# State-space slots with their own fixed order on TensorE, and decay sums brought by DMA instead of made by matmuls

## Chip, core and metric

The kernel runs on one core of a Trainium2 chip. The metric is the device time of one execution in microseconds (us); lower is better. A core has five engines with a queue of instructions each: TensorE (PE, with weight loads as PEld), VectorE (DVE), ScalarE (ACT), GpSimd (POOL) and SyncE (SP), which here only issues DMAs. Each works off its queue in order, and waits for others through semaphores.

## What is computed

Two layers over 1024 latent and 256 context positions of width 1024: gated windowed attention, then a gated bidirectional state-space mixer (SSD), each with modulated normalization and a residual. The change touches only the second. For each of 8 groups (4 heads of 64 channels each, a state of 128) it projects, convolves over 5 neighbours, applies silu, and scans in 8 chunks of 128 positions, in both directions, from states that the context leaves behind:

```python
def ssd_chunk_pass(xdt, da, bm, cm, h0, want_y):
    a_cs = jnp.cumsum(da, axis=2)
    a_last = a_cs[:, :, -1]
    decay_to_end = jnp.exp(a_last[:, :, None] - a_cs)
    states = jnp.einsum('bcsgn,bcsgr,bcsgrp->bcgrpn', bm, decay_to_end, xdt)
    ...
    diff = a_cs[:, :, :, None] - a_cs[:, :, None, :]
    lmat = jnp.exp(jnp.where(lower, diff, -jnp.inf))
    cb = jnp.einsum('bcqgn,bcsgn->bcqsg', cm, bm)
    y_diag = jnp.einsum('bcqsg,bcqsgr,bcsgrp->bcqgrp', cb, lmat, xdt)
    y_off = jnp.einsum('bcqgn,bcgrpn,bcqgr->bcqgrp', cm, h_prev, jnp.exp(a_cs))
```

`da` is the step size times a negative rate, so `lmat` holds, for each pair of positions of a chunk, how much of one has decayed by the other: the decays. Both directions are added, with a skip term, multiplied by silu(z), normalized within the group and projected back to width 1024.

## The kernel before

A product of two float32 matrices is made of three matmuls of rounded halves (high x high, high x low, low x high). Products of the scan itself run in plain float32, which the trace shows as two matmul instructions for each in the program.

The method `ssd` starts with `ssd_consts`: step sizes, their running sums `acs` in both directions and logarithms of step sizes, all with 64 rows (2 directions x 32 heads); these go to DRAM (`acs_d`, and `v_d` with the logarithm minus the sum), split in two halves by `rows`, and, transposed chunk by chunk, to SBUF.

Then come 64 **slots**, one for each chunk of each group. A slot of group g makes, on TensorE: the score matrix `pcb` (C times B, 128x128); the inter-chunk part `po`, from the forward state `hf` and the stored backward state `hb`; the update `S` of `hf`; the diagonal part `yd` (4 matmuls, one for each head, with the decays times the scores `M` as weights); and two transpositions of the finished rows of the slot before (the tail), which go to DRAM as `uN`. Beside its own work a slot holds a share of **front(g+1)**: the projections of the next group, four weight tiles of 128 channels (B, x, x, C: `bT`, two `cacc`, `cT`) of 48 matmuls of 512 columns, 24 of 256 columns for the context (not for C), and 192 matmuls of 256 columns for z. In group 7, with no next group, the fill is the output projection `ssd_out`.

`fill(x)` runs front until a share of its estimated cost is spent; `SEGS` sets the shares. What follows a projection (5 conv taps on ACT and DVE, tanh, product, and for B and x the transpositions `natural` back into PSUM with ACT copies) is put into a list, `post`, of which one step is taken for each 0.5 us of estimated matmul time; the transpositions are held back by `LATE` further microseconds of it. `states(g+1)` makes the states of the next group from its context and then the backward states, chunk by chunk, each with a matmul into the one buffer `psD`, a DVE addition and POOL products (`xw`, `decay`); `tick()` takes one step of it, three times a slot.

The **decays** of slot n+1 are made in slot n. SP loads 12 rows of `acs_d` and `v_d` into `rraw` (three DMAs), ACT rounds them into `rrow`, and for each half (2 heads) two matmuls of 256 columns add sums and logarithms for both directions into PSUM; DVE's `copy_predicated` picks the direction by position (`before`), and ACT's Exp writes `M`.

The order in which the program is written is not the order of the queues: a scheduler with a timing model of its own places each engine's instructions as it takes them to become ready. What is printed below are the functions that the change touches, as they stood.

Of the kernel before, what the change touches and what calls it, by code (L numbers as in the profile page):

```python
# [9 lines left out]
F32 = mybir.dt.float32  # L10
BF16 = mybir.dt.bfloat16
F32R = mybir.dt.float32r
# [33 lines left out]
    cacc=2, cctx=1, bT=2, cT=2, xn4=4, xn2=1, bn4=4, bn2=1, sz=2, xw=2, hf=2, hx=2, M=2, y2=1, xs=1, uT=2, pj2=2, psX=3, sk=2, dg=2,  # L46
# [13 lines left out]
LATE = 3.0  # L60
SEGS = (1.5, 2.0, 2.0, 2.2, 2.2)
# [42 lines left out]
class Kernel:  # L104
# [762 lines left out]
    def ssd_consts(self, p):  # L867
# [18 lines left out]
        self.dtb = t(p, [P, NCH, 32], F32, "dtb")  # L886
        self.eal = t(p, [P, 64, NT], F32, "eal")

        self.acs_d = t(dr, [2, 64, LAT], F32, "acs")
        self.v_d = t(dr, [2, 64, LAT], F32, "vrow")  # L890
# [28 lines left out]
        for lo, n, chunks in ((0, 768, (0, 1, 2, 3, 8, 9)), (768, 512, (4, 5, 6, 7))):  # L919
# [24 lines left out]
            def rows(dst, src):  # L944
                h = t(q, [64, 512], F32R, "rowh", 2)
                l = t(q, [64, 512], F32R, "rowl", 2)
                nc.scalar.copy(h, src[:, :512])
                nc.vector.tensor_sub(l, src[:, :512], h)
                for x, y in enumerate((h, l)):
                    nc.sync.dma_start(dst[x, :, chunks[0] * P : chunks[0] * P + 512], y.bitcast(F32))  # L950

            rows(self.acs_d, acs)
# [11 lines left out]
            rows(self.v_d, ln)  # L964
# [6 lines left out]
            for b, c in enumerate(chunks):  # L971
                sl = slice(b * P, (b + 1) * P)
                pt = t(ps, [P, 256], F32, "psX")
                nc.tensor.transpose(pt[:, 0:64], dd[:, sl], self.ident[:64, :64])
                nc.scalar.copy(self.dtdec[:, c, :], pt[:, 0:64])
                if c < NCH:
                    nc.tensor.transpose(pt[:, 64:128], acs[:, sl], self.ident[:64, :64])
# [16 lines left out]
    def silu(self, raw, acc):  # L994

        nc = self.nc
        return [lambda: nc.scalar.activation(raw, acc, AF.Tanh),
                lambda: nc.vector.scalar_tensor_tensor(acc, in0=raw, scalar=1.0, in1=acc, op0=ALU.add, op1=ALU.mult)]

    def front(self, g, st, post, first=None):  # L1000
# [31 lines left out]
        def natural(raw, acc, dst, o, n):  # L1032
# [12 lines left out]
            return [(LATE, steps)]  # L1045
# [9 lines left out]
        for n, (x, kind) in enumerate(tiles):  # L1055
# [4 lines left out]
            if nat:  # L1060
# [6 lines left out]
                post.extend(self.taps(x, raw, acc, 0, CTX, CTX) + self.silu(raw, acc) + natural(raw, acc, [(st[nat[0]][2], 0, 2)], nat[1], 2))  # L1067
# [46 lines left out]
    def ssd(self, c0):  # L1114
# [11 lines left out]
        rraw = t(ps2, [32, 6, P], F32, "rraw")  # L1126
        rrow = t(ps2, [P, 6, P], F32R, "rrow")
        nc.sync.dma_start(rraw, a["rrow"].rearrange("p (r n) -> p r n", r=6))
        nc.vector.memset(rrow.bitcast(F32), 0.0)
# [60 lines left out]
        def load_rows(n):  # L1190
            g, c = divmod(n, NCH)
            cs = slice(c * P, (c + 1) * P)
            ar = self.acs_d.rearrange("h (d k) n -> (h d) k n", d=2)[:, 4 * g : 4 * g + 4, cs]
            nc.sync.dma_start(rraw[0:4, :4], ar)
            for d in range(2):
                nc.sync.dma_start(rraw[4 + 8 * d : 12 + 8 * d, 4 + d], self.v_d[:, hd(d, g), cs])

        def round_rows(n):
            nc.scalar.copy(rrow[:32], rraw)
            if n + 1 < G * NCH:  # L1200
                load_rows(n + 1)

        def decays(n, M, half):

            o = t(ps, [P, 512], F32, "psX").rearrange("p (d r n) -> p d r n", d=2, r=2)
            for d in range(2):
                nc.tensor.matmul(o[:, d], rrow[:, 4 + d], rrow[:, 2 * half : 2 * half + 2], start=True, stop=True)
            nc.vector.copy_predicated(o[:, 0], self.before.unsqueeze(1).broadcast_to([P, 2, P]), o[:, 1])
            nc.scalar.activation(M[:, 2 * half : 2 * half + 2], o[:, 0], AF.Exp)

        def slot(n, st, M, fill, tick, last):

            g, c = divmod(n, NCH)
            cs = slice(c * P, (c + 1) * P)
            xc = X(st, c).rearrange("p (r h) -> p r h", r=R)
            if n + 1 < G * NCH:
                round_rows(n + 1)
            pcb = t(ps, [P, 512], F32, "psX")[:, :P]
            nc.tensor.matmul(pcb, st["bT"][:, cs], st["cT"][:, cs], start=True, stop=True)
            po = t(ps, [P, 512], F32, "psX")  # L1220
            nc.tensor.matmul(po[:, :256], st["cT"][:, cs], flat(st["hf"]), start=True, stop=True)
            nc.tensor.matmul(po[:, 256:], st["cT"][:, cs], flat(st["hb"][c]), start=True, stop=True)
            nc.vector.tensor_tensor(M, M, pcb.unsqueeze(1).broadcast_to([P, R, P]), op=ALU.mult)
            if c < NCH - 1:
                S = t(ps, [P, 512], F32, "psX")
                hn = t(ps2, [P, R, HP], F32, "hf")
                decay(hn, st["hf"], g, c, 0)
                nc.tensor.matmul(S[:, :256], B(st, c), flat(st["xw"]), start=True, stop=True)
                nc.vector.tensor_add(hn, hn, S[:, :256].rearrange("p (r h) -> p r h", r=R))
                st["hf"] = hn  # L1230
            y2 = t(ps2, [P, 2, R, HP], F32, "y2")
            nc.vector.tensor_tensor(y2, po.rearrange("p (d r h) -> p d r h", d=2, r=R),
                                    self.eacs[:, c, :].rearrange("p (d q) -> p d q", d=2)[:, :, 4 * g : 4 * g + 4].unsqueeze(3).broadcast_to([P, 2, R, HP]), op=ALU.mult)
            fill(0)
            xs = t(ps2, [P, R, HP], F32, "xs")
# [3 lines left out]
            nc.vector.scalar_tensor_tensor(sk, in0=self.dtb[:, c, 4 * g : 4 * g + 4], scalar=dg, in1=self.dsk[:, 4 * g : 4 * g + 4], op0=ALU.mult, op1=ALU.add)  # L1239
            y = ys[n % 2]  # L1240
            yf = y[:, :256]
            yv = yf.rearrange("p (r h) -> p r h", r=R)
            nc.gpsimd.tensor_tensor(xs, xc, sk.unsqueeze(2).broadcast_to([P, R, HP]), op=ALU.mult)  # L1243
            nc.gpsimd.tensor_tensor(yv, y2[:, 0], y2[:, 1], op=ALU.add)
            nc.gpsimd.tensor_tensor(yv, yv, xs, op=ALU.add)
            yd = t(ps, [P, 512], F32, "psX")
            for r in range(R):
                nc.tensor.matmul(yd[:, r * HP : (r + 1) * HP], M[:, r], X(st, c)[:, r * HP : (r + 1) * HP], start=True, stop=True)
            if self.tail is not None:
                self.tail(t(ps, [P, 512], F32, "psX"))  # L1250
            fill(1)
            nM = None
            if n + 1 < G * NCH:
                nM = t(ps2, [P, R, P], F32, "M")
                decays(n + 1, nM, 0)
# [3 lines left out]
            nc.scalar.activation(y2.rearrange("p d r h -> p (d r h)")[:, :257], y[:, :257], AF.Square, scale=1.0 / 16.0, accum_out=ss)  # L1259
            nc.gpsimd.tensor_tensor(ss, ss, self.half, op=ALU.pow)  # L1260
            fill(2)
            if nM is not None:
                decays(n + 1, nM, 1)
            nc.scalar.activation(yf, yf, AF.Copy, scale=ss)
            if c < NCH - 2:
                st["xw"] = xweight(st, g, c + 1, 0)
            tick()
            fill(3)
            tick()
            fill(4)  # L1270
            tick()

            def tail(pt):
# [6 lines left out]
            self.tail = tail  # L1280
            return nM
# [3 lines left out]
        load_rows(0)  # L1285
# [14 lines left out]
        M = t(ps2, [P, R, P], F32, "M")  # L1300
        round_rows(0)
        for half in range(2):
            decays(0, M, half)
        st["xw"] = xweight(st, 0, 0, 0)
        self.tail = None
        with ExitStack():
            for g in range(G):
# [3 lines left out]
                else:  # L1311
                    cf.close()
                    post.flush()
                    work, total = self.ssd_out(self.pool("out", ctx=c0, side="right"), [(p, [P, 2, 512], F32, "xn4")] * 4, p, ps2, post), OUT * 0.85
                spent = 0.0
                chain = None

                def run(until):
                    nonlocal spent
# [6 lines left out]

                def tick():
                    nonlocal chain
                    if g < G - 1 and 1 in nst:
                        chain = chain or states(g + 1, nst)  # L1330
                        next(chain, None)

                for c in range(NCH):
                    def fill(x):
                        run(total * (c + sum(SEGS[: x + 1]) / sum(SEGS)) / NCH)
                    M = slot(g * NCH + c, st, M, fill, tick, g == G - 1)
                if g < G - 1:
                    run(1e9)
                    while 1 not in nst or not nst["sz"]:
                        post.pop()  # L1340
                    chain = chain or states(g + 1, nst)
                    for _ in chain:
                        pass
                    nst["xw"] = xweight(nst, g + 1, 0, 0)
                    st = nst
            self.tail(t(ps, [P, 512], F32, "psX"))
# [222 lines left out]
def layout(i):  # L1569
# [34 lines left out]
    rr = np.zeros((32, 6, P), np.float32)  # L1604
    for x in range(4):
        for r in range(R):
            rr[4 + 4 * x + r, r] = 1.0
        rr[x, 4 + x % 2] = 1.0
    d["rrow"] = rr.reshape(32, -1)
# [30 lines left out]
```

## Time and profile before

| | |
|---|---|
| median of 3 runs | 1858.76 us (1854.27 to 1859.07) |
| the profiled execution | 1859.22 us, span of its trace 1857.5 us |
| attention layer, to the first matmul of the first front | to about 753 us |
| first front, states and constants | about 753 to 870 us |
| slots of groups 0 to 6 | about 870 to 1630 us |
| slots of group 7, between matmuls of the output projection | about 1630 to 1770 us |
| rest of the output projection, final norm | 1770 to 1857 us |
| granted TensorE clock, whole run | 0.985 |

In the profile a row of a group ends with busy time, mean duration, the engine's idle time just ahead of these instructions and what ended it. In a timeline a row is start, duration, engine, line, operation, written tile and tiles read; in square brackets the idle time before it. A matmul starts before the one ahead of it has ended, so the cost of a matmul on TensorE is the distance from start to start, not its duration.

### The profile page before, as it was taken

Reading aid. Unit: us, or ns where it says so; the run is one execution under the profiler, and the core shown is the slowest. Engines: PE = TensorE matmul, PEld = TensorE weight load, DVE = VectorE, ACT = ScalarE, POOL = GpSimd, SP = SyncE. Lnnn points to the kernel's source line nnn. Section 1 sums busy time; section 2 is a strip of 40 time slices with the busy share of each in tenths; the row PEclk is TensorE's granted clock in tenths of the full one; section 3 lists DMA queues with packets and bytes.
Section 4 is the critical chain, followed back from the end, with each engine's and each line's share of the span. In section 5 each row is a group of like instructions: output and inputs, shape, how many; then the busy total and the mean of one; then the engine's idle time right before and its main releaser. Section 6 shows DMA issues by size and latency. Waiting matters only on the chain. (4 is left out here: it accounts for less than half of the span.)

```text
span 1857.5 us, 29739 instructions
## 1 busy us (share of the span) xinstructions
PE 1779.2 (96%) x10684; PEld 1539.4 (83%) x10684; DVE 1175.8 (63%) x2208; ACT 902.6 (49%) x1858; POOL 732.1 (39%) x1007
## 2 busy tenths in 40 slices
PE   6999999999999999889999999999999999999997
PEld 4797877788898787668898898989889898988886
DVE  3564438877787665773766657576665757754743
ACT  3522336677788664652444435344443534543532
POOL 2441137654466466003352443525244352532411
PEclk9999999999999999989999999999999999999998
DMA  7767866443354445221111111111111111433552
GB/s 293 279 165 252 263 179 153 105 118 96 88 137 120 129 125 191 64 61 36 30 45 47 34 47 34 48 33 40 52 33 47 34 47 35 156 109 95 175 162 71
DMA packets 145491, 196.30 MB, mean 106 GB/s; under 512 B 15392, under 2 KB 84896, under 8 KB 144320
## 3 DMA queue, kind: packets, MB, share of 16 engines
q1 hardware_dynamic: 111280, 175.76, 29.8%
q0 software_dynamic: 34064, 18.65, 5.6%
q8 instruction: 84, 1.38, 0.3%
q14 instruction: 63, 0.52, 0.1%
HBM read 158.73 MB, written 35.92 MB: 105 GB/s over the span
## 5 line engine op out<-in xcount | busy, mean ns | idle before, releaser
L226 PE MATMUL pj<-uH,wh 128*128 128x256 f32 (+1 forms) x652 | 232.3, 356 | 6.4 <-DVE xn L1528 1.9
L228 PE MATMUL pj<-uH,wl 128*128 128x256 f32 (+1 forms) x652 | 219.5, 337 | 0.0
L227 PE MATMUL pj<-uL,wh 128*128 128x256 f32 (+1 forms) x652 | 219.3, 336 | 0.0
L1148 POOL TENSOR_TENSOR xw<-xn,dtdec 128x256 f32<-128x256 f32 x144 | 105.9, 738 | 209.4 <-PE psD L1171 100.9
L1073 PE MATMUL pj<-uH,wh 128*128 128x512 f32 x512 | 172.7, 407 | 1.1 <-ACT xn L1040 1.1
L1073 PE MATMUL pj<-uH,wl 128*128 128x512 f32 x512 | 172.0, 405 | 0.0
L1073 PE MATMUL pj<-uL,wh 128*128 128x512 f32 x512 | 168.6, 399 | 0.0
L214 POOL TENSOR_TENSOR wl<-wr,wh 128x512 fp32r<-128x512 f32 x92 | 121.3, 1322 | 94.4 <-ACT wh L212 91.4
L1098 PE MATMUL pj<-wh,uH 128*128 128x256 f32 x512 | 154.0, 301 | 0.0
L702 DVE TENSOR_TENSOR pl<-pt,ph 128x512 fp32r<-128x512 f32 x168 | 114.2, 687 | 60.5 <-ACT ph L701 59.8
L1098 PE MATMUL pj<-wh,uL 128*128 128x256 f32 x512 | 150.8, 294 | 0.0
L1098 PE MATMUL pj<-wl,uH 128*128 128x256 f32 x512 | 150.4, 294 | 0.0
L226 PEld LDWEIGHTS pj<-uH,wh 128*128 128x128 f32 x652 | 124.2, 190 | 28.6 <-issue 7.8
L676 DVE CUSTOM_DVE_ANT_0 sm<-S,mask,nsink 128x640 f32<-128x640 f32 (+2 forms) x160 | 118.9, 771 | 33.8 <-PE S L673 19.7
L1277 ACT ACTIVATE uT<-psX,nw 128x128 f32<-128x128 f32 x128 | 47.0, 367 | 189.0 <-PE psX L1276 188.0
L228 PEld LDWEIGHTS pj<-uH,wl 128*128 128x128 f32 x652 | 123.7, 190 | 14.2 <-issue 0.8
L227 PEld LDWEIGHTS pj<-uL,wh 128*128 128x128 f32 x652 | 124.5, 191 | 10.1 <-issue 1.1
L212 ACT CAST wh<-wr 128x512 fp32r<-128x512 f32 (+1 forms) x132 | 84.7, 645 | 93.6 <-PE pj L227 73.3
L701 ACT CAST ph<-pt 128x512 fp32r<-128x512 f32 x168 | 97.6, 586 | 62.4 <-PE pt L697 56.2
L678 ACT ACTIVATE sm<-sm,nm 128x640 f32<-128x640 f32 (+2 forms) x160 | 118.5, 741 | 17.7 <-DVE nm L676 14.9
L1243 POOL TENSOR_TENSOR xs<-xn,sk 128x256 f32<-128x256 f32 x64 | 42.1, 658 | 185.2 <-DVE sk L1239 184.0
L1073 PEld LDWEIGHTS pj<-uL,wh 128*128 128x128 f32 x512 | 96.0, 189 | 20.0
(346 smaller groups left out, 5059.5 us busy)
## 6 DMA issues: line engine op xcount, KB each, us to landing
wr<-w_x SPq DMA_DIRECT2D x32, 512.0 KB
wr<-w_sk SPq DMA_DIRECT2D x24, 512.0 KB
wr<-wg SPq DMA_DIRECT2D x44, 256.0 KB
qs<-q POOLq DMA_DIRECT2D x40, 256.0 KB, 4.0
wr<-wo SPq DMA_DIRECT2D x40, 256.0 KB
wada<-w_ad SPq DMA_DIRECT2D x8, 1024.0 KB
wr<-wq SPq DMA_DIRECT2D x32, 256.0 KB
wl<-w_ada SPq DMA_DIRECT2D x32, 256.0 KB
```

Source lines behind the costliest of these rows:

```text
L212: nc.scalar.copy(h, raw)
L214: (eng or nc.vector).tensor_tensor(l, raw, h, op=ALU.subtract)
L226: self.nc.tensor.matmul(ps, lh, rh, start=first and i == 0, stop=False)
L227: self.nc.tensor.matmul(ps, lh, rl, start=False, stop=False)
L228: self.nc.tensor.matmul(ps, ll, rh, start=False, stop=last and i == n - 1)
L676: nc.vector.tensor_tensor_reduce(out=sm[:, :W], in0=Sv, in1=self.mask[:, m0 : m0 + W], scale=-SCALE, scalar=self.nsink[:, 4 * j + r : 4 * ...
L678: nc.scalar.activation(sm[:, :W], sm[:, :W], AF.Exp, bias=nm[:, r : r + 1], scale=-1.0, accum_out=sums[:, r : r + 1])
L701: nc.scalar.copy(ph, ptf)
L702: nc.vector.tensor_sub(pl, ptf, ph)
L1073: nc.tensor.matmul(raw[:, 512 * i : 512 * i + 512], l[:, k, :], r[i][:, k, :], start=k + y == 0, stop=k == KT - 1 and y == 2)
L1098: nc.tensor.matmul(pj[:, c], l, r[:, k, :], start=c % 2 + q + k + y == 0, stop=c % 2 == 1 and q == 1 and k == 3 and y == 2)
L1148: nc.gpsimd.tensor_tensor(xw, X(st, c).rearrange("p (r h) -> p r h", r=R), self.dtdec[:, c, hd(d, g)].unsqueeze(2).broadcast_to([P, R, HP] ...
```

## The change

Decays: `v_d`, the split `rows`, `rraw`, `rrow` and the four decay matmuls of each slot go. `acs_d` now holds the sums unsplit. For each slot and direction one DMA of 256 KB brings the 4 rows of sums to all 128 partitions (`fd` forward, `bd` backward, two buffers each), since the sums of the key position are on the partition axis and can be given as a bias. These biases are made in `ssd_consts` by one more transposition for each of the 8 chunks (`vf`, the logarithm minus the forward sum, and `vo`, the difference of the directions). POOL adds `vo` to `bd`, DVE picks by `before` from SBUF, and ACT runs Exp per head with bias `vf`, in place; `M` is then the buffer `fd`.

Order: the slot is cut into functions (`scores`, `inter`, `state`, `diagonal`, `finish`) and turned round: an iteration now starts with the diagonal part of slot n, and makes scores, inter and state of slot n+1 between the fills. From the end of the first slot's preparation to the start of group 7, `pin` ties every TensorE instruction to the one written before it, so there the scheduler can't reorder TensorE (the other engines it still can). `LATE` is 9.5 in place of 3.0 for latent transpositions, 7.5 for those of the context, and the states are stepped by spent cost (1.6 us apart for the four of the context, which start before the second x tile's latent part is ready; then 2.4) in place of `tick`.

```diff
-LATE = 3.0
-SEGS = (1.5, 2.0, 2.0, 2.2, 2.2)
+LATE = 9.5
+BD = 2
+SEGS = (2.6, 2.4, 2.2, 2.25)
...
-            rows(self.acs_d, acs)
+            nc.sync.dma_start(self.acs_d[0][:, chunks[0] * P : chunks[0] * P + 512], acs[:, :512])
...
-            rows(self.v_d, ln)
...
+                    nc.tensor.transpose(pt[:, 192:256], ln[:, sl], self.ident[:64, :64])
+                    nc.scalar.copy(self.vf[:, c, :], pt[:, 192:224])
+                    nc.vector.tensor_sub(self.vo[:, c, :], pt[:, 224:256], self.vf[:, c, :])
...
+    def pin(self, first):
+        traced = self.nc.cur_bb.bb.instructions
...
+            if i.engine == mybir.EngineType.PE:
+                if last is not None:
+                    self.tc.add_manual_dep(i, last.name, ... NoSync ..., reason="pin")
+                last = i
...
-        def round_rows(n):
-            nc.scalar.copy(rrow[:32], rraw)
-        def decays(n, M, half):
-            o = t(ps, [P, 512], F32, "psX").rearrange("p (d r n) -> p d r n", d=2, r=2)
-            for d in range(2):
-                nc.tensor.matmul(o[:, d], rrow[:, 4 + d], rrow[:, 2 * half : 2 * half + 2], start=True, stop=True)
-            nc.vector.copy_predicated(o[:, 0], self.before.unsqueeze(1).broadcast_to([P, 2, P]), o[:, 1])
-            nc.scalar.activation(M[:, 2 * half : 2 * half + 2], o[:, 0], AF.Exp)
+        def load_rows(n, d):
+            if n < G * NCH:
+                g, c = divmod(n, NCH)
+                x = rows[n, d] = t(ps2, [P, R, P], F32, ("fd", "bd")[d])
+                nc.sync.dma_start(x, self.acs_d[:, hd(d, g), c * P : (c + 1) * P].broadcast_to([P, R, P]))
+        def decays(n):
+            g, c = divmod(n, NCH)
+            x, y = [rows.pop((n, d)) for d in range(2)]
+            nc.gpsimd.tensor_tensor(y, y, self.vo[:, c, 4 * g : 4 * g + 4].unsqueeze(2).broadcast_to([P, R, P]), op=ALU.add)
+            nc.vector.copy_predicated(x, self.before.unsqueeze(1).broadcast_to([P, R, P]), y)
+            for r in range(R):
+                nc.scalar.activation(x[:, r], x[:, r], AF.Exp, bias=self.vf[:, c, 4 * g + r : 4 * g + r + 1])
+            load_rows(n + BD, 1)
+            return x
...
                 for c in range(NCH):
-                    M = slot(g * NCH + c, st, M, fill, tick, g == G - 1)
+                    ss = diagonal(n, st, cur)
+                    if tail:
+                        tail()
+                    load_rows(n + 2, 0)
+                    if n + 1 < G * NCH:
+                        cur = {"M": decays(n + 1)}
+                    tail = finish(n, ss)
+                    fill(0)
...
+                    scores(n + 1, st, cur)
+                    fill(1)
+                    if c < NCH - 1:
+                        fs = state(n + 1, st, cur)
+                        next(fs)
+                        inter(n + 1, st, cur)
+                        fill(2)
+                        for _ in fs:
+                            pass
...
+                    fill(3)
```

Three places show what moved. The first is TensorE at the decays of a slot in group 0 (`psX` at `rrow` is a half of the decays, `psX` at `xn` the diagonal part, `psX` at `ident` a tail, `pj` and `psD` at `ident` natural transpositions). Before:

```order
L1037 MATMUL pj_2309_9778<-ident_63,bT_9779 128x128 x4
L1248 MATMUL psX_9873<-xn_2209_9008,M_9790 128x64 x4
L1276 MATMUL psX_9878<-ident_63,y_2207_9001 128x128
L1037 MATMUL psD_9739<-ident_63,cctx_9777 128x128 x2
L1207 MATMUL psX_9895<-rrow_8998 128x256 x2
L1037 MATMUL pj_2309_9778<-ident_63,bT_9779 128x128 x2
L1207 MATMUL psX_9926<-rrow_8998 128x256 x2
L1037 MATMUL pj_2309_9778<-ident_63,bT_9779 128x128 x2
L1276 MATMUL psX_9878<-ident_63,y_2207_9001 128x128
```

And now, TensorE in the same group, from the state update of a slot to the transpositions of the first x tile:

```order
L1250 MATMUL psX_10180<-xw_10178,bn_2208_9016 128x256
L1082 MATMUL pj_2364_10148<-uH_2057_8255,wl_10033 128x512
L1082 MATMUL pj_2364_10148<-uH_2144_8675,wl_10033 128x512
L1082 MATMUL pj_2364_10148<-uH_2057_8255,wh_10031 128x512
L1082 MATMUL pj_2364_10148<-uH_2144_8675,wh_10031 128x512
L1082 MATMUL pj_2364_10148<-uL_2058_8256,wh_10031 128x512
L1082 MATMUL pj_2364_10148<-uL_2145_8676,wh_10031 128x512
L1082 MATMUL pj_2364_10148<-uH_2057_8255,wl_10033 128x512
L1082 MATMUL pj_2364_10148<-uH_2144_8675,wl_10033 128x512
L1044 MATMUL pj_2336_9960<-ident_63,cacc_9961 128x128 x8
```

The decay matmuls are gone, and the eight transpositions of a tile stand in one piece, eight projection matmuls behind the state update. The second place is VectorE ahead of those transpositions, now:

```order
L1219 TENSOR_TENSOR fd_9996<-fd_9996,psX_10159 128x512
L1222 ISA xs_10162,dg_10163<-psX_10159,ident_63 128x128
L1222 ISA dg_10163 128x1
L986 SCALAR_TENSOR_TENSOR cacc_9961<-pj_2336_9960,cw_8723,cacc_9961 128x1023
L986 SCALAR_TENSOR_TENSOR cctx_10147<-psD_10087,cw_8723,cctx_10147 128x255
L1224 SCALAR_TENSOR_TENSOR sk_10165<-dtb_8737,dg_10163,dsk_8731 128x4
L1235 TENSOR_TENSOR y_2374_10186<-psX_10183,eacs_8735 128x512
L986 SCALAR_TENSOR_TENSOR cacc_9961<-pj_2336_9960,cw_8723,cacc_9961 128x1022
L986 SCALAR_TENSOR_TENSOR cctx_10147<-psD_10087,cw_8723,cctx_10147 128x255
L1251 TENSOR_TENSOR hf_10181<-hf_10181,psX_10180 128x256
L986 SCALAR_TENSOR_TENSOR cctx_10147<-psD_10087,cw_8723,cctx_10147 128x254
L994 SCALAR_TENSOR_TENSOR cacc_9961<-pj_2336_9960,cacc_9961 128x1024
```

The last row makes what TensorE transposes; the addition to `hf`, which waits for the state update on TensorE, stands two rows ahead of it. The third place is TensorE ahead of slot 0, where the states of group 0 end (`psD` at `xw`). Before:

```order
L1219 MATMUL psX_9718<-cT_9333,bT_9049 128x128
L1171 MATMUL psD_9549<-xw_9526,bn_2212_9011 128x256
L1221 MATMUL psX_9720<-hf_2250_9403,cT_9333 128x256
L1073 MATMUL pj_2309_9778<-uH_2057_8255,wh_9643 128x512
L1073 MATMUL pj_2309_9778<-uH_2144_8675,wh_9643 128x512
L1073 MATMUL pj_2309_9778<-uL_2058_8256,wh_9643 128x512
```

And now:

```order
L1107 MATMUL pj_2263_9560<-wh_9418,uL_2145_8676 128x256
L1217 MATMUL psX_9709<-cT_9337,bT_9053 128x128
L1176 MATMUL psD_9613<-xw_9590,bn_2207_9015 128x256
L1176 MATMUL psD_9634<-xw_9611,bn_2207_9015 128x256
L1176 MATMUL psD_9659<-xw_9632,bn_2207_9015 128x256
L1250 MATMUL psX_9720<-xw_9718,bn_2207_9015 128x256
L1232 MATMUL psX_9725<-hf_2249_9465,cT_9337 128x256
L1259 MATMUL psX_9732<-xn_2204_9012,fd_9004 128x64 x4
L1233 MATMUL psX_9725<-hb_2280_9661,cT_9337 128x256
L1071 MATMUL psD_9761<-uH_1735_7025,wh_9642 128x256
```

Before, projection matmuls of the next group stood between the last states; now the last three states follow each other, and the next group's first matmul stands behind the first diagonal part.

More of the change, by code (lines that the diff above doesn't have):

```diff
@@ L45 @@
     oraw=3, h1=2, h1k=8, wada=8, sqa=1,
[L46 removed]
+    cacc=2, cctx=1, bT=2, cT=2, xn4=4, xn2=1, bn4=4, bn2=1, sz=2, xw=2, hf=2, hx=2, fd=2, bd=2, y2=1, xs=1, uT=2, pj2=2, psX=3, sk=2, dg=2,
 )
@@ L1299, in ssd @@
             pass
[L1300 to L1305, printed above, removed]
+        cur = {"M": decays(0)}
+        scores(0, st, cur)
+        for _ in state(0, st, cur):
+            pass
+        inter(0, st, cur)
+        tail = None
+        traced = nc.cur_bb.bb.instructions
+        first = traced[-1]
         with ExitStack():
@@ L1325, in run @@
                         post.run(cost)
[L1327 to L1331, printed above, removed]
+                        if g < G - 1 and "ctx" in nst:
+                            chain = chain or states(g + 1, nst)
+                            if spent - mark > (1.6 if steps < 4 else 2.4) and (steps < 4 or 1 in nst):
+                                next(chain, None)
+                                steps += 1
+                                mark = spent
@@ L1337, in ssd @@
+                    fill(3)
                 if g < G - 1:
                     run(1e9)
[L1339 to L1346, printed above, removed]
+            tail()
         for _ in work:
```

161 lines of the change are left out of this document (81 added, 80 removed).

## The prediction

> **What bounds the kernel now.** First the page's busy times, then the same by stage, since an average over 1858 us says little about the slots.
>
> ```profile
> span 1857.5 us, 29739 instructions
> PE 1779.2 (96%) x10684; PEld 1539.4 (83%) x10684; DVE 1175.8 (63%) x2208; ACT 902.6 (49%) x1858; POOL 732.1 (39%) x1007
> ```
>
> ```profile
> 800.00:870.00 70.00, 65.80 (x403) 59.14 (x402) 38.09 (x46) 24.49 (x54) 11.79 (x18) 0.91 0.14 40
> 870.00:1640.00 770.00, 764.98 (x4814) 690.19 (x4813) 511.36 (x939) 341.88 (x693) 311.72 (x465) 1.00 0.17 50
> 1640.00:1770.00 130.00, 128.62 (x626) 107.12 (x625) 73.05 (x123) 55.45 (x105) 43.77 (x52) 1.00 0.41 126
> ```
>
> Behind each window and its length stand the busy times of PE, PEld, DVE, ACT and POOL, the granted TensorE clock, the DMA engines' share and GB/s. In the slots TensorE works 765 of 770 us at full clock; VectorE 511, ScalarE 342, GpSimd 312. Busy PE alone proves little, as matmuls overlap; so next the waits of TensorE from 850 to 1640 us, with total, number and the longest:
>
> ```profile
> PE psD L1171 <- POOL xw L1148: 3.4, 7, 0.5
> PE pj L1488 <- DVE wl L1424: 1.6, 1, 1.6
> ```
>
> These are all of them: one of 0.5 us per group, at its first state, and one at the output projection. So its own work sets the time of the slots. What leaves TensorE there shortens the kernel by its full price, until a wait takes its place; what is added on the others costs nothing as long as TensorE isn't made to wait.
>
> **What leaves TensorE.** A piece of TensorE's timeline in group 3:
>
> ```profile
> 1246.38 0.62 PE L1073 MATMUL pj<-uH,wl 128*128 128x512 f32 x2
> 1246.84 0.40 PE L1207 MATMUL psX<-rrow 128*128 128x256 f32 x2
> 1247.08 0.27 PE L1276 MATMUL psX<-ident,y 128*128 128x128 f32 x1
> 1247.19 0.60 PE L1037 MATMUL pj<-ident,cacc 128*128 128x128 f32 x4
> ```
>
> Two decay matmuls take 0.24 us from start to start (1246.84 to 1247.08), a 512-column matmul 0.23 (0.46 for two), a 128-column transposition's instruction 0.11. A slot has two such pairs, 64 slots have 128: 128 x 0.24 = 30.7 us less. No other matmul of the slots goes or comes. In `ssd_consts` 8 transpositions are added:
>
> ```profile
> 800.00:810.00 10.00, 9.63 (x51) 8.74 (x50) 8.95 (x11) 7.20 (x28) 0.00 (x0) 0.52 0.23 57
> 794.67 0.62 ACT L947 CAST rowh<-w 64x512 fp32r<-64x512 f32 x1 [2.18 <-DVE w L943]
> 797.34 0.68 DVE L948 TENSOR_TENSOR rowl<-w,rowh 64x512 fp32r<-64x512 f32 x1 [0.41 <-ACT rowh L947]
> 799.60 0.36 PE L977 MATMUL psX<-ident,w 64*128 64x64 f32 x1 [6.89 <-ACT dtdec L975]
> ```
>
> By the last row such a transposition is 0.36 us at most; 8 are under 3 us, partly in a stretch where TensorE waits anyway: +1 us. The same rows show a gain. TensorE sits idle for 6.9 us before these transpositions, behind a chain on ACT and DVE to which the split into halves belongs (rows at 0.62 and 0.68 us, four of each, now gone), and the first window shows the clock at 0.52 in the 10 us behind the gap, which is up to 4.8 us lost. The new order also has projection matmuls between the transpositions. From 0 to 10 us less, then; I take 4, near the two casts and two subtractions of the later half (2.6 us) and some of the clock, since how far the gap shrinks is unknown. [...]
>
> **What the fixed order adds.** TensorE now waits wherever its next written instruction isn't ready. I walked one group's order against durations of these rows (timeline and groups):
>
> ```profile
> 1199.61 0.69 DVE L1223 TENSOR_TENSOR M<-M,psX 128x512 f32<-128x512 f32 x1
> 1200.22 0.28 DVE L1237 CUSTOM_DVE_ANT_0 xs<-psX,ident 128x128 f32<-128x128 f32 x1
> 1200.43 0.08 DVE L1237 DVE_READ_ACCUMULATOR2_ANT dg<- 128x1 f32 x1
> 1200.55 0.22 DVE L1239 SCALAR_TENSOR_TENSOR sk<-dtb,dg,dsk 128x4 f32<-128x4 f32 x1
> ...
> 1206.99 0.59 PE L1171 MATMUL psD<-xw,bn 128*128 128x256 f32 x2
> 1207.42 0.59 PE L1228 MATMUL psX<-xw,bn 128*128 128x256 f32 x2
> 1207.69 0.42 DVE L1183 TENSOR_TENSOR hb<-hb,psD 128x256 f32<-128x256 f32 x1 [5.05 <-PE psD L1171]
> 1207.85 1.00 PE L1248 MATMUL psX<-xn,M 128*128 128x64 f32 x8
> 1208.05 0.42 DVE L1229 TENSOR_TENSOR hf<-hf,psX 128x256 f32<-128x256 f32 x1
> ```
>
> ```profile
> L990 DVE SCALAR_TENSOR_TENSOR cacc<-pj,cw,cacc 128x1022 f32<-128x1022 f32 (+1 forms) x56 | 71.5, 1277 | 7.9 <-ACT cacc L986 7.8
> L1208 DVE COPY_PREDICATED psX<-before,psX 128x256 f32<-128x256 int32 x126 | 53.2, 423 | 69.7 <-PE psX L1207 69.1
> L990 DVE SCALAR_TENSOR_TENSOR cctx<-psD,cw,cctx 128x254 f32<-128x254 f32 (+1 forms) x84 | 39.8, 473 | 0.3
> L1232 DVE TENSOR_TENSOR y<-psX,eacs 128x512 f32<-128x512 f32 x64 | 43.8, 685 | 18.2 <-PE psX L1222 18.0
> L1257 DVE TENSOR_TENSOR y<-y,sz 128x256 f32<-128x256 f32 x64 | 29.4, 460 | 0.8
> L1256 DVE TENSOR_TENSOR y<-y,psX 128x256 f32<-128x256 f32 x64 | 26.6, 416 | 42.9 <-PE psX L1248 24.9 <-POOL y L1245 18.1
> L998 DVE SCALAR_TENSOR_TENSOR cacc<-pj,cacc 128x1024 f32<-128x1024 f32 x14 | 17.0, 1212 | 0.0
> ```
>
> *First x tile.* From the end of a diagonal part to its eight transpositions TensorE has 4 tail instructions (0.44 us), 18 context matmuls (256 columns, half of 0.23 each: 2.1), 30 projection matmuls (6.9), the scores (half of a 256-column float32 product, which is 0.43 from 1206.99 to 1207.42: 0.22), `po` (0.86) and `S` (0.43): 10.9 us. In the same stretch VectorE has the two operations on `y` (0.42 and 0.46), `copy_predicated`, four taps (5.1) and four of the context (1.9), scores with their small operations (0.61, 0.33 and 0.22 start to start), `po` (0.69), the addition to `hf` (0.42) and the product behind the tanh (1.21): with 0.69 for the predicated copy 12.0 us, less about 0.08 where one follows another at once (0.69 against 0.61 at 1199.61), some 1.0: 11.0. It begins 0.2 us late (1208.05 against 1207.42 and 0.43) and waits about 0.4 us for the rows of `fd`. So it is done 0.7 us behind TensorE: 7 groups x 0.7 = +5 us. The same walk leaves VectorE 0.5 us ahead at `bT` and 2.5 us ahead at the second x tile: nothing there.
>
> The predicated copy, from SBUF and 512 columns wide, isn't in the trace: at least one of 256 columns (0.42), at most two (0.85); 0.69 is the 0.69 of the other 512-column operations. The rows of `fd` are asked for when the diagonal part has read their buffer. Their landing is bounded by two rows, SP's longest wait for a small transfer and the only 256 KB one whose landing the page gives:
>
> ```profile
> SPq L1194 <- DMA rraw<-acs: 10.3, 6, 1.9
> qs<-q POOLq DMA_DIRECT2D x40, 256.0 KB, 4.0
> ```
>
> Between 1.9 and 4.0 us I take 2.5, as SP's queue holds nothing that waits long in front of these loads by the new order. The decays themselves are made a slot ahead of their use, so a late landing doesn't hold `M`; it holds what stands behind `copy_predicated` on VectorE, the taps. The scheduler placed it there. DMA traffic is no matter: 128 loads of 256 KB are 34 MB in 900 us, 37 GB/s on top of 50, and the slots of group 7 run with 126.
>
> *Start of slot 0.* The last three states of group 0 now follow each other with one buffer, and nothing between. Behind the last z matmul stand, each waiting for the one before: tanh of z, its product (1.2, as the product of the same size above), an addition to a state (0.42), 0.22, the split of a weight, the next addition (0.42), POOL's decay, the last addition (0.42). The last row gives POOL's product as minimum, median and maximum in ns.
>
> ```profile
> L1106 ACT ACTIVATE sz<-pj 128x1024 f32<-128x1024 f32 x16 | 16.3, 1021 | 12.8 <-PE pj L1098 12.7
> L1017 DVE TENSOR_TENSOR wl<-wr,wh 128x1024 fp32r<-128x1024 f32 x42 | 52.1, 1239 | 0.3 <-ACT wh L1013 0.2
> L1153 POOL TENSOR_TENSOR hb<-hb,eal 128x256 f32<-128x256 f32 x56 | 37.8, 675 | 3.6 <-DVE hb L1183 3.6
> ...
> L1148 POOL TENSOR_TENSOR xw<-xn,dtdec x144: 609/615/1612, 843.3 to 1705.7; 128x256 f32<-128x256 f32 x144
> ```
>
> That is 1.0 + 1.2 + 0.4 + 0.2 + 1.2 + 0.4 + 0.7 + 0.4 = 5.5 us, in which TensorE has scores, three states, `S`, the forward half of `po` and a diagonal part: 0.2 + 5 x 0.43 + 1.0 at most = 3.4. Left: +2.1, with handovers 2.5 us (0 if the tanh comes early, 6 if each handover costs as the 0.7 us from 1206.99 to 1207.69).
>
> *First state of a group.* The 0.5 us wait shown above ends with the old place; at the new one a copy on ACT and a product on POOL (0.61 us) stand against seven matmuls, 1.6 us. Between 3.4 less (none) and 3 more (0.4 late on top of the old wait); I take 1 less.
>
> Other edits cost nothing: POOL's addition (two 256-column operations of 0.61, so 1.2 us a slot, 77 in all) fits in the 458 us in which POOL is idle in the slots; ACT swaps a cast and two Exp for four shorter ones with 428 us idle; two DMA issues of SP replace three. Their cover is TensorE's work, and without it each would be on the path.
>
> **Sum.** Against the profiled execution's own 1859.2 us (span 1857.5 and 1.7 around it; the median 1858.8 stands 0.5 below): -30.7 + 1 - 4 + 5 + 2.5 - 1 = -27.2. That is 1832 us.
>
> **Rivals.** *Held on the shared way into SBUF, or rows at 4.0 us (1847).* Ops that read two tensors from SBUF on VectorE and POOL seem to hold each other:
>
> ```profile
> L1257 DVE TENSOR_TENSOR y<-y,sz x64: 409/424/1057, 893.8 to 1760.4; 128x256 f32<-128x256 f32 x64
> ```
>
> Minimum, median, maximum, and with them POOL's product above: usually 0.42 and 0.61 us, now and then 0.6 to 1.0 us more. The predicated copy read PSUM and now reads SBUF, beside a new POOL operation of 1.2 us. If it lost that each slot, VectorE would be 1.9 us late at the first x tile and 0.7 at `bT`: 7 x 2.6 = 18 in place of 5, 1845 us. Rows at 4.0 instead of 2.5 us give 2.2 and 1.0, 22 in place of 5: 1849. Against both: the medians sit at the minimum. [...]
>
> *Late rows (slower, 1874).* `fd` is loaded only once its buffer is free, on a queue with 512 KB weight loads. If a load lands 5.5 us behind the diagonal part, VectorE stands for 3 us more at its predicated copy in each slot, and is late by 3.7, 2.5 and 0.5 us at the three tiles: 7 x 6.7 = 47 in place of 5, 1874 us. It decides from the point where 0.7 + x and x - 0.5 make up 4.6 us a group (27 / 7 plus the 0.7 counted): x = 2.2, a landing of 4.7 us. For it: the 4.0 above, and that VectorE's queue is full in that stretch; against it: the DMA engines are busy 17%.
>
> *No change (1859).* What leaves TensorE comes back as waits of 0.5 us a slot at places I took as covered.
>
> **How the numbers follow.** The forecast has 0.60, the held case 0.15, late rows 0.18, no change 0.07. By its own terms the forecast runs from 1821 (no late tile, the whole 10 us at the constants) to 1843 (no gain there, 6 at slot 0, 3 more at the states). To leave out no more than 2 in 10 the range goes over the held case and no change: 1820 to 1864. A measurement of this kernel tells 0.3%, 5.6 us, from nothing: faster 0.73 (forecast and nearly all of the held case), same 0.08, slower 0.19.
>
> **What would show it.** Right: the group's period shrinks by 3 us or more; TensorE's waits list the transpositions of `cacc` behind DVE L994 at well under 2 us each, and nothing per slot; VectorE's wait at `copy_predicated` is for DMA and short. Wrong: waits of TensorE that come 56 times; a wait at `copy_predicated` over 2 us; a clock under 1.00 in the slots; the predicated copy or POOL's addition with a median far above 0.7 and 1.2 us.

## Result, and the profile after

The change makes the kernel slower: 2009.68 us (2006.47 to 2012.48, 4 runs) against 1857.38 us for the kernel before, a ratio of 1.083 (95% interval 1.0814 to 1.0847), or 152 us more. The forecast was 1832 us, and its range ended at 1864.

The page of the changed kernel first: busy times, two groups, and the issues of the rows.

```profile
span 2010.8 us, 29193 instructions
PE 1822.1 (91%) x10436; PEld 1543.3 (77%) x10436; DVE 1177.0 (59%) x2147; ACT 897.5 (45%) x1926; POOL 783.9 (39%) x1071
...
L1206 POOL TENSOR_TENSOR bd<-bd,vo 128x512 f32<-128x512 f32 x64 | 68.2, 1066 | 341.0 <-DMA bd<-acs 307.2
...
L1207 DVE COPY_PREDICATED fd<-before,bd 128x512 f32<-128x512 int32 x64 | 48.1, 752 | 163.5 <-DMA fd<-acs 159.5
...
fd<-acs SPq DMA_DIRECT2D x64, 256.0 KB, 4.8
bd<-acs SPq DMA_DIRECT2D x64, 256.0 KB, 4.7
```

TensorE's share fell from 96% to 91%. The two new operations are about as long as expected (0.75 us for the copy against 0.69, 1.07 for the addition against 1.2). But POOL stands 307 us ahead of its addition and VectorE 160 us ahead of its copy, 4.8 and 2.5 us a slot, for rows whose loads are written one slot (`fd`) and two slots (`bd`) ahead of these operations. By stage (window and length, busy PE, PEld, DVE, ACT and POOL, granted clock, DMA share, GB/s), the 910 us in which the slots of groups 0 to 6 now lie:

```profile
870.00:1780.00 910.00, 796.66 (x4512) 688.11 (x4511) 507.42 (x871) 333.48 (x736) 355.59 (x524) 0.94 0.26 70
```

Two things go wrong in it: TensorE is idle for 113 us (before: 5 of 770), and the rest runs at a mean clock of 0.94 (before: 1.00). Its waits there of over 1 us in all, with total, number and the longest:

```profile
PE psX L1280 <- ACT uT L1281: 33.6, 55, 3.3
PE pj L1044 <- DVE cacc L994: 21.8, 7, 3.7
PE pj L1044 <- ACT xn L1047: 17.0, 14, 2.5
PE psD L1176 <- POOL xw L1153: 15.0, 12, 2.5
PE pj L1044 <- DVE bT L994: 11.1, 7, 2.2
PE psD L1176 <- DVE hb L1188: 8.9, 10, 1.6
PE pj L1044 <- ACT bn L1047: 4.7, 7, 0.7
```

They are of two kinds. In rows 1, 3 and 7 TensorE's next transposition waits until ACT has read an earlier one from the same PSUM tile: the tail in nearly every slot, the halves of a natural three times a group. Rows 2, 4, 5 and 6 are producers on VectorE and POOL that come late.

Why they are late shows in a piece of the timeline in group 3, first VectorE, then POOL, then SP's issues, each with start and duration:

```profile
1219.95 0.42 DVE L1264 TENSOR_TENSOR y<-y,sz 128x256 f32<-128x256 f32 x1
1220.30 1.22 DVE L994 SCALAR_TENSOR_TENSOR cacc<-pj,cacc 128x1024 f32<-128x1024 f32 x1
1225.04 0.73 DVE L1207 COPY_PREDICATED fd<-before,bd 128x512 f32<-128x512 int32 x1 [3.52 <-DMA fd<-acs]
1225.66 0.67 DVE L1219 TENSOR_TENSOR fd<-fd,psX 128x512 f32<-128x512 f32 x1
```

```profile
1221.06 0.55 POOL L1267 TENSOR_TENSOR ss<-ss,half 128x1 f32<-128x1 f32 x1 [2.52 <-ACT y L1266]
1230.61 1.04 POOL L1206 TENSOR_TENSOR bd<-bd,vo 128x512 f32<-128x512 f32 x1 [9.00 <-DMA bd<-acs]
1231.61 1.59 POOL L1226 TENSOR_TENSOR xs<-xn,sk 128x256 f32<-128x256 f32 x1
1233.17 1.18 POOL L1153 TENSOR_TENSOR xw<-xn,dtdec 128x256 f32<-128x256 f32 x2
```

```profile
1219.42 0.36 SPq L1201 DMA_DIRECT2D fd<-acs  x1
1221.26 0.36 SPq L1282 DMA_DIRECT2D uN<-uT  x1
1225.83 0.36 SPq L1201 DMA_DIRECT2D bd<-acs  x1
```

`fd` is asked for at 1219.42 and VectorE's copy starts at 1225.04, 5.6 us later; the copy frees `bd`, its load goes out at 1225.83 (from 870 to 1750 us SP waits 195 us for that copy), and POOL's addition starts at 1230.61, 4.8 us later. Each operation stands right behind the load that it needs, and both loads lie one after the other in one slot, with both queues held. The order of the queues says why. On POOL, from the end of slot 1 on, in the changed kernel (`ss` is the last POOL operation written in a slot; the buffer numbers of `bd` tell which slot's it is):

```
L1267 TENSOR_TENSOR ss_2319_9859<-ss_2319_9859,half_2158_8733 128x1
L1206 TENSOR_TENSOR bd_2343_10004<-bd_2343_10004,vo_2163_8739 128x512
L1226 TENSOR_TENSOR xs_2325_9898<-xn4_2204_9012,sk_2327_9901 128x256
```

`bd_2282` belongs to the decays written at this place, those of slot 2; `bd_2343` is that of slot 5. And on VectorE the copy for slot 3 stands ahead of the scores of slot 2:

```
L1207 COPY_PREDICATED fd_2322_9869<-before_2166_8742,bd_2295_9750 128x512
L1219 TENSOR_TENSOR fd_2294_9742<-fd_2294_9742,psX_2324_9895 128x512
```

The scheduler has put POOL's addition three slots ahead of its written place and VectorE's copy one, behind the load that the freed buffer allows. So the lead that the two buffers give is used up by the consumer running ahead; nothing of it is left to cover the landing.

### The profile page after: what moved, and what is told of

It reads as the page before. It is cut to its first block, busy times and chain, and to the rows that moved or that the text cites. A ratio compares the mean times of both kernels' runs of the same rounds, so it can differ in the third digit from the quotient of the medians.

```text
span 2010.8 us, 29193 instructions
## 1 busy us (share of the span) xinstructions
PE 1822.1 (91%) x10436; PEld 1543.3 (77%) x10436; DVE 1177.0 (59%) x2147; ACT 897.5 (45%) x1926; POOL 783.9 (39%) x1071
## 5 line engine op out<-in xcount | busy, mean ns | idle before, releaser
L1206 POOL TENSOR_TENSOR bd<-bd,vo 128x512 f32<-128x512 f32 x64 | 68.2, 1066 | 341.0 <-DMA bd<-acs 307.2
L1082 PE MATMUL pj<-uH,wh 128*128 128x512 f32 x512 | 187.6, 435 | 0.7 <-ACT bn L1047 0.7
L1082 PE MATMUL pj<-uH,wl 128*128 128x512 f32 x512 | 182.1, 426 | 0.0
L1082 PE MATMUL pj<-uL,wh 128*128 128x512 f32 x512 | 174.6, 419 | 0.0
L1107 PE MATMUL pj<-wh,uL 128*128 128x256 f32 x512 | 156.3, 305 | 0.0
L1107 PE MATMUL pj<-wh,uH 128*128 128x256 f32 x512 | 149.7, 292 | 1.1 <-ACT xn L1047 1.1
L1153 POOL TENSOR_TENSOR xw<-xn,dtdec 128x256 f32<-128x256 f32 x144 | 88.9, 626 | 154.9 <-ACT vf L975 81.4
L1209 ACT ACTIVATE fd<-fd,vf 128x128 f32<-128x128 f32 x256 | 81.9, 390 | 143.1 <-DVE fd L1207 143.1
L1207 DVE COPY_PREDICATED fd<-before,bd 128x512 f32<-128x512 int32 x64 | 48.1, 752 | 163.5 <-DMA fd<-acs 159.5
L228 PEld LDWEIGHTS pj<-uL,wh 128*128 128x128 f32 x652 | 124.4, 191 | 10.0 <-issue 1.1
```

What stands on the lines that cost most here:

```text
L228: self.nc.tensor.matmul(ps, lh, rl, start=False, stop=False)
L1082: nc.tensor.matmul(raw[:, 512 * i : 512 * i + 512], l[:, k, :], r[i][:, k, :], start=k + y == 0, stop=k == KT - 1 and y == 2)
L1107: nc.tensor.matmul(pj[:, c], l, r[:, k, :], start=c % 2 + q + k + y == 0, stop=c % 2 == 1 and q == 1 and k == 3 and y == 2)
L1153: nc.gpsimd.tensor_tensor(xw, X(st, c).rearrange("p (r h) -> p r h", r=R), self.dtdec[:, c, hd(d, g)].unsqueeze(2).broadcast_to([P, R, HP] ...
```

## Experiments

Theory L: late rows, because the scheduler hoists their consumers. Theory S: the fixed order sets dependent transpositions of one PSUM tile side by side. All times are medians; the kernel before measured 1856 to 1858 beside them.

**e1 to e4: one piece at a time.** e1 ties each of the two operations to the last one written before it on its engine:

```diff
+    def place(self):
+        i, *past = reversed(self.nc.cur_bb.bb.instructions)
+        last = next(k for k in past if k.engine == i.engine)
+        self.tc.add_manual_dep(i, last.name, ... NoSync ..., reason="place")
...
             nc.gpsimd.tensor_tensor(y, y, self.vo[...]..., op=ALU.add)
+            self.place()
             nc.vector.copy_predicated(x, self.before..., y)
+            self.place()
```

> The changed kernel, but POOL's addition to bd and DVE's predicated copy may not be put ahead of the last POOL or DVE instruction written before them; loads, buffers and TensorE's order stay. Theory L (late rows: the scheduler hoists both one to three slots, straight behind a load that lands 4.8 us later, and both queues stand there): POOL's 285 us and DVE's 146 us of waits for DMA fall under 20 us each, TensorE's waits at the transpositions of cacc and bT (21.8 and 11.1) and at the states (14.8 and 8.1) mostly go, and the time falls by 50 to 90 us, to 1920 to 1960. Theory S (TensorE's fixed order puts two dependent instructions of one PSUM tile next to each other): the DMA waits may go, but the 29.8 us at the tails and 21.7 at the natural halves stay, and the time moves under 15 us.

e2 leaves that and writes transpositions ahead of the copies that read them, in the tail and in `natural`:

```diff
                 for e in range(2):
                     nc.tensor.transpose(pt[:, e * P : (e + 1) * P], yf[...], self.ident)
+                for e in range(2):
                     nc.scalar.activation(uT[:, e], pt[:, e * P : (e + 1) * P], ...)
...
             for d, lo, hi in dst:
                 steps.append(lambda lo=lo, hi=hi: tr(lo, hi))
+            for d, lo, hi in dst:
                 steps.append(lambda d=d, lo=lo, hi=hi: ev(d, lo, hi))
```

> The changed kernel, but both transpositions of a tail, and all eight of a natural, are written ahead of the ACT copies that read them. Theory S: the 29.8 us at the tails and 21.7 us at the natural halves go, with some of the clock's loss: 50 to 75 us less, 1935 to 1960. Theory L: these waits go, but TensorE only comes earlier to instructions whose producers are late, whose waits grow in their place: under 20 us less, 1990 or more.

e3 drops the line `self.pin(first)`.

> The changed kernel without the fixed order on TensorE: the scheduler places all. Theory S: it puts other matmuls between the dependent ones, the waits at tails and naturals go, 50 us or more less, under 1960. Theory L: POOL and DVE still stand behind the loads (over 200 us together); the time falls under 25 us or rises, 1985 or more.

e4 is the kernel before, slots and order untouched, with the change's `load_rows`, `decays` and constants.

> The kernel before with its order, its LATE and its ticks, no fixed order; only the decays are made as in the change (rows by DMA two slots ahead, POOL's addition, copy from SBUF, four Exp). Theory S: the late rows cost nothing where the scheduler orders TensorE, and the 30.7 us of decay matmuls are won: 1825 to 1840. Theory L: POOL and DVE stand behind the loads here too, TensorE waits for states or transpositions: 1870 or more.

Measured: e1 1902.95, e2 1986.31, e3 1943.75, e4 1975.81 us. e1 gives back 107 us, more than theory L asked for (50 to 90), and e2 23, a little more than it allowed (under 20). e4 settles that the decays alone, without any of the new order, cost 119 us. e3 gives back 66 us and so falls where theory S had it (under 1960): the scheduler separates most of the pairs. But POOL still waits 215.6 us and VectorE 98.9 us for rows, as theory L had it, and the kernel stays 87 us behind the one before. In e1 the rows land no sooner (first two rows, median to landing), VectorE and POOL no longer wait for these rows, and 47.5 of TensorE's 59 us of waits are theory S (rows 1, 2 and 4 of the second block):

```profile
fd<-acs SPq DMA_DIRECT2D x64, 256.0 KB, 5.0
bd<-acs SPq DMA_DIRECT2D x64, 256.0 KB, 5.0
```

```profile
PE psX L1288 <- ACT uT L1289: 33.3, 55, 1.6
PE pj L1050 <- ACT xn L1053: 9.5, 14, 0.7
PE psD L1182 <- POOL xw L1159: 5.3, 7, 0.8
PE pj L1050 <- ACT bn L1053: 4.7, 7, 0.7
```

So it isn't the landing of 4.8 us that makes rows late, but the place of their consumers. One tail of e1, transposition, copy, transposition:

```profile
1020.58 0.28 PE L1288 MATMUL psX<-ident,y 128*128 128x128 f32 x1
...
1020.90 0.37 ACT L1289 ACTIVATE uT<-psX,nw 128x128 f32<-128x128 f32 x1 [3.13 <-PE psX L1288]
...
1021.32 0.33 PE L1288 MATMUL psX<-ident,y 128*128 128x128 f32 x1 [0.46 <-ACT uT L1289]
```

The second writes other columns than ACT reads, and still waits for it, here 0.46 us; no run tried to go without that wait. From start to start the pair takes 0.74 us, where two transpositions in a row take 0.11 each: 0.63 us more, of which the profile's idle time shows 0.46; the mean of such a wait is 0.6 us (33.3 over 55).

**e5 to e8: both, and each half of the change alone.**

> Both edits at once: POOL's addition and DVE's copy kept at their written place (first edit), and tails and naturals with all transpositions ahead of their copies (second edit). With the rows in time, the 47.5 us of waits that are left at tails (33.3, 55 times) and natural halves (9.5 and 4.7, 21 times) should go, and some 0.2 us for each of the 76 gaps that TensorE needs to fill up again: 1903 less 63, 1840 us (1832 to 1852). If something else still is late in each slot, the waits move there: 1875 or more.

e6 keeps the changed order and brings back `rows`, `rraw`, `rrow` and the four decay matmuls of the kernel before:

```diff
-                    load_rows(n + 2, 0)
                     if n + 1 < G * NCH:
-                        cur = {"M": decays(n + 1)}
+                        cur = {"M": t(ps2, [P, R, P], F32, "M")}
+                        decays(n + 1, cur["M"], 0)
                     tail = finish(n, ss)
                     fill(0)
+                    if n + 1 < G * NCH:
+                        decays(n + 1, cur["M"], 1)
+                    if n + 2 < G * NCH:
+                        round_rows(n + 2)
```

> The change's order (slots cut and turned, fixed on TensorE, LATE, state steps), but the decays made on TensorE as before: half by half, one right behind the tail, one behind the first fill; no rows of 256 KB. If late rows and the dependent pairs are two separate costs, the pairs' 47.5 us and 15 us of refilling stand here without the late rows: 1905 to 1930, and no waits of POOL or DVE for DMA. If the order by itself costs nothing, under 1870.

> The kernel before in its own order, with the decays by DMA (as in the earlier run of the decays alone, 1976 us), but POOL's addition and DVE's copy kept at their written place. If the hoisting is the cause, POOL and DVE no longer stand at loads, and the 30.7 us of the decay matmuls come out: 1825 to 1845. If the rows or the new operations cost by themselves (traffic, SBUF reads, POOL's 1.05 us), 1865 or more.

> The order alone with decays on TensorE (as in e6), and tails and naturals with all transpositions ahead of their copies. If the dependent pairs are what the order costs, 1850 to 1868, level with the kernel before; if the order has other costs, 1885 or more.

Measured: e5 **1827.78** (ratio to before 0.9852, 0.9831 to 0.9873), e6 1924.09, e7 **1829.86** (0.9864, 0.9849 to 0.9879), e8 1855.87 us (0.9998, 0.9987 to 1.0009). e6, e7 and e8 fall in the range of the theory that has both causes, e5 4 us below it. Decays off TensorE are worth 28 us in the new order (e8 less e5) and 26 in the old (e7) once their consumers stay in place; the new order is worth nothing (e8), and 68 us less than nothing with the pairs in it (e6 less e8). TensorE's largest wait from 870 to 1640 us in e6, and that in e8:

```profile
PE psX L1291 <- ACT uT L1292: 33.0, 51, 1.4
PE psD L1185 <- DVE hb L1197: 2.8, 2, 2.2
```

In e5 TensorE is busy in the slots as it was before, and these are all of its waits from 870 to 1640 us:

```profile
870.00:1640.00 770.00, 766.43 (x4715) 686.29 (x4716) 526.90 (x906) 344.81 (x780) 373.54 (x539) 1.00 0.33 91
```

```profile
PE psX L1268 <- DVE fd L1228: 3.1, 1, 3.1
PE pj L1535 <- DVE sz L1125: 0.5, 1, 0.5
PE psD L1183 <- DVE hb L1195: 0.2, 1, 0.2
PE psX L1241 <- DVE y L1272: 0.2, 1, 0.2
```

**e9 to e12: which queue, and what the fixed order is worth.** e9 and e10 are e5 with `place()` behind POOL's addition alone, or behind VectorE's copy alone; e11 and e12 are e1 and e5 without `self.pin(first)`.

> Pairs edit, and only POOL's addition kept at its written place; DVE's copy is free to move but needs that addition first. Which of the two queues that stand at the loads costs the 158 us between 1986 (pairs alone) and 1828 (pairs, both kept)? If POOL's (252 us of waits, with state inputs xw, hb and the skip term behind it): within 10 us of 1828, and DVE's wait for DMA is gone too, as its copy can't overtake the addition. If DVE's (133 us, conv taps behind it) has a cost of its own: 1860 or more.

> Pairs edit, and only DVE's copy kept at its written place; POOL's addition may still be hoisted to two slots ahead, right behind its load. If POOL's stand is what costs: POOL still waits over 200 us for DMA and the time is 1900 or more. If DVE's stand was the cost (the step as the prediction had it, at DVE alone): under 1850, with POOL waiting at no cost.

> The change with both operations kept at their written place, and no fixed order on TensorE (tails and naturals as in the change). If the fixed order is worth nothing by itself and only exposes the dependent pairs: 1825 to 1845, as the scheduler sets other work between them. If the order must be fixed for the gain: 1860 or more. If the scheduler leaves the pairs adjacent: near 1903.

> Both operations kept at their written place, pairs edit, no fixed order on TensorE. With the fixed order this was 1828, without it and without the pairs edit 1846 with 21.5 us of waits, most behind the ACT copies of natural halves (L1053). If those copies are what is left there: 1825 to 1835, and the fixed order is worth nothing. If the fixed order itself earns something: 1840 to 1850.

Measured: e9 1827.29, e10 1858.72, e11 1845.64, e12 1830.42 us. e9 is e5: with POOL's addition in place VectorE's copy can't run ahead either. e10 went neither way. POOL still stands for 250 us, and that costs 31 us, 17 of it at a state of the next group, about once a group:

```profile
POOL bd L1213 <- DMA bd<-acs: 250.0, 53, 9.0
```

```profile
PE psD L1183 <- POOL xw L1160: 17.1, 8, 3.0
```

So of the 158 us between e2 and e5 POOL's stand alone makes 31; the other 127 need VectorE's copy to run ahead too. VectorE's stand without POOL's was not to be had, since its copy needs POOL's addition. A third buffer for the rows, the other way to lead further, was not run. e11 and e12: the fixed order earns nothing in either form (1846 against 1903 with the pairs side by side, 1830 against 1828 with them split); it only takes away the scheduler's means of setting other work between dependent transpositions. The best version is e5 or e9, 28 to 31 us under the kernel before and 182 under the change; e7 and e12 are 2 to 3 us behind them, too little for these runs to tell from nothing.

## Why the prediction was wrong

**Where the step failed: the landing of the rows, and what waits for them.** The prediction had VectorE's copy right behind its own load ("The scheduler placed it there.") and took "2.5" us for the landing (upper bound: 4.0), which left "about 0.4 us" of waiting a slot. Measured are a landing of 4.8 us and 2.5 us of waiting a slot (159.5 us). For POOL it put nothing: the addition "fits in the 458 us in which POOL is idle". That compares busy times, but the addition stands in front of `xw`, `hb` and `xs`, on a load that goes out only when VectorE's copy has freed the buffer, and POOL waits there for 307 us. Nor did it ask why the copy stands behind its own load: kept at their written place, both operations find the same rows in time (e1, e5), though these land in 5.0 us.

Its rival of late rows had the sign and the threshold, 4.7 us; the landing was just past it. But it priced the lateness at 47 us against 5. With the pairs out of the way it is 158 us (e2 less e5). In e2, the stage from 870 to 1780 us and TensorE's three largest waits in it:

```profile
870.00:1780.00 910.00, 804.35 (x4658) 707.42 (x4657) 511.60 (x897) 335.19 (x759) 359.65 (x535) 0.95 0.28 75
```

```profile
PE pj L1044 <- DVE cacc L994: 27.8, 7, 4.4
PE psD L1177 <- POOL xw L1154: 25.9, 7, 5.5
PE pj L1044 <- DVE bT L994: 21.7, 7, 3.9
```

All of TensorE's waits there make 105 us, and the clock of 0.95 some 45 (an estimate: 0.05 of the 910 us). The price left out POOL's wait, the second load behind the first, and the clock.

**The second failed step: "Other edits cost nothing" of the order, and the walk through one group.** It compared the durations of queues, and did not ask whether neighbours on TensorE depend on each other. The rival of "waits of 0.5 us a slot at places I took as covered" describes the tails (0.6 us each in e1), with 0.07 of chance; but it let them only cancel the gain. They cost 68 us without the late rows (e6 less e8), 75 with rows in time (e1 less e5), and 23 on top of late rows, where TensorE would only have waited elsewhere.

**Right: what leaves TensorE.** 128 x 0.24 = 30.7 us less, with the small terms -27.2. With both faults mended, e5 comes out 28.2 us under the kernel before (1855.98 beside it), e7 26. So the mechanism of the forecast was there; two costs of 226 us together (158 and 68) hid it, and where both were present they overlapped. That the sum of -27.2 agrees with e5 to 1 us is partly luck: without its +5 for the first x tile, which e5 does not show, it would be -32.

**The small terms.** *First x tile, +5:* 21.8 us in the change; in e5 no wait at `cacc`. It was counted behind a copy that waited for rows. *Start of slot 0, +2.5:* e5 waits 3.1 us there once, right in size. *First state, -1:* the 0.5 us a group are gone in e5, twelve waits with 15.0 us in the change. *Constants, -4:* the gap of 6.9 us became one of 4.7 in the change and 4.6 in e5, at the natural transpositions of `bT` instead, and the clock in 800 to 810 us went from 0.52 to 0.66 in e5; what of it was won was not measured apart. *Added transpositions, +1:* not told apart either.

**The rival "Held on the shared way into SBUF"** did not show: in the change the copy's durations are 726 / 741 / 1142 ns (minimum, median, maximum), POOL's addition 1037 / 1039 / 2082. Now and then one takes longer, as in the prediction's maxima, but the medians stay near the minimum. One such pair from the trace of the kernel before: VectorE's product of `y` and `sz` at 966.18 us, both from SBUF, takes 0.67 us beside a POOL product (from 965.95, 0.62 us), against a median of 0.42, while its addition of `psD` from PSUM to `hb` at 965.40 takes 0.42 beside another (from 965.38, 0.62 us). What the two share was not shown.

**Its own signs** were the right ones: waits that come 56 times (55 at the tails), a long stand at `copy_predicated`, and a clock under 1.00 in the slots all showed.

## What to carry to other kernels

A load that is issued a slot or two early helps only if its consumer stays where it was written: where a scheduler may hoist the consumer, it ends up right behind its load on an in-order queue, and everything behind it on that queue pays for the landing (here 4.8 us). So read which slot's tile an instruction handles, not just where its line stands in the queue, and tie the consumer down (here one dependency on POOL's addition turned 1986 into 1827 us). And before an engine's order is fixed by hand, look for neighbours that wait for each other through another engine: with the transpositions ahead of the copies that read them TensorE did not wait there (e8), alternated with them it lost 68 us at some 76 places (e6 less e8).

## What was unexpected of the hardware

The clock halved behind short stalls of TensorE. In e10, a stall of 1.99 us ahead of 1164.07, and the clock (third column from the end) in the microseconds behind it:

```profile
1164.07 0.70 PE L1183 MATMUL psD<-xw,bn 128*128 128x256 f32 x2 [1.99 <-POOL xw L1160]
```

```profile
1164.00:1165.00 1.00, 0.93 (x6) 0.88 (x7) 0.20 (x1) 0.00 (x0) 1.00 (x3) 1.00 0.77 295
1165.00:1166.00 1.00, 1.00 (x8) 0.89 (x7) 0.26 (x2) 0.00 (x0) 1.00 (x3) 0.75 0.33 131
1166.00:1167.00 1.00, 1.00 (x6) 1.00 (x6) 1.00 (x2) 0.00 (x0) 1.00 (x2) 0.50 0.00 0
1167.00:1168.00 1.00, 1.00 (x6) 1.00 (x6) 0.96 (x2) 0.00 (x0) 1.00 (x3) 0.50 0.09 16
1168.00:1169.00 1.00, 1.00 (x7) 1.00 (x6) 0.90 (x1) 0.00 (x0) 0.26 (x1) 0.54 0.00 0
1169.00:1170.00 1.00, 1.00 (x9) 0.95 (x9) 0.25 (x1) 0.00 (x0) 0.27 (x1) 1.00 0.00 0
```

By these rows it is at half for about 3.4 us (0.5, 1, 1 and 0.9), beginning some 1.4 us after TensorE is at work again. In e2 a stall of 3.03 us, ahead of the transpositions of `bT` at 1538.58, was followed by 1.00 in every microsecond up to 1543. Stalls of some 0.6 us in every slot did nothing: e1 and e6 run their slots at 1.00 (870 to 1700 and 870 to 1640 us). So the length of a stall alone didn't tell here whether the clock would fall: 1.99 us was followed by the fall, 3.03 us was not, and no run shows what decides. In the changed kernel the clock was at half 14 times between 870 and 1780 us, for 3.4, 6.8 or 10.2 us each and 109 us together, every time beside a stall of 1.5 to 3.7 us; half of 109 in 910 us is the 0.06 that took it to 0.94.
